# A hybrid decoder layer on one core: a different number of k-pairs by seven products, and partial sums of weights added by transfers

## The chip, the core and the metric

The kernel runs on one NeuronCore of a Trainium2 chip. Five instruction streams run side by side: TensorE (PE, with its weight loads shown as PEld), VectorE (DVE), ScalarE (ACT), GpSimd (POOL) and SyncE (SP, which only issues transfers here). They meet through semaphores. The metric is the device time of one execution in microseconds; the median of three runs is given, with the lowest and the highest beside it.

## The reference, cut to what matters

One layer of a decoder, 256 tokens, width 2048, in float32. What matters here is only which large products there are and what follows what:

```python
proj = h @ w_in[i]                       # x_r, g_r, q, k, v, gate_r, gate_a
...
y_r = y_r @ w_rnn_out[i]                 # 2816 x 2048
o = stick_breaking_attention(q, k, v)
y_a = o... @ w_attn_out[i]               # 2048 x 2048
mix = sigmoid(gate_r) * y_r + sigmoid(gate_a) * y_a
x = x + mix @ w_o[i]
gu = rmsnorm(x, g_ffn[i]) @ w_ffn_gu[i]  # 2048 x 11264
x = x + (silu(g) * u) @ w_ffn_down[i]    # 5632 x 2048
x = x + sigmoid(rmsnorm(x, g_ple[i]) @ w_ple_gate[i]) * (p[i] @ w_ple_proj[i])
```

## The kernel before

**Tiles.** Everything is cut into 128. The 256 tokens are two token tiles (0 and 1); a weight matrix is cut into k-tiles (rows) and into groups of 1024 columns, each group being two halves of 512 columns. A float32 value is split into a high and a low part, and `prod` (L613) multiplies one token tile by one 128 x 512 weight piece in three matmuls: high by high, high by low, low by high (L617, L618, L619). What is a weight in the layer is the moving operand here, and the activations are what PE loads.

**Plain k-tiles and pairs.** A plain k-tile needs four products: two token tiles by two column halves. So two plain k-tiles need eight. Two k-tiles can instead be taken as a pair, as a 2 x 2 block product with seven multiplications. It needs sums of weight pieces (`T1`, `T2`, `T3`, `T4` and the like) and sums of activations, which `half_sums` makes (four sums of 128 columns on DVE, then a split into two parts). `pairs_of(name)` says which pairs of a product are done in this way. The first two pairs go as strings in the list of slots ("11", "T1", "21", "22", "T2", "T3", "T4"; each covers both pairs, so each slot has two products); a further pair goes as ("S", 1, p) to ("S", 4, p), four slots with two, two, two and one products.

**Lists of slots.** A group (1024 columns of one product) follows a list: `SEVEN` has two pairs and twelve plain k-tiles, `SEVEN3` three pairs and ten plain ones, `LONG` is `SEVEN3` with six more, and `ONE` has one pair and ten plain ones. Before the change the recurrent output `ro`, `v`, all eleven groups `gu` of the feed-forward's first product, the down parts `dn0` and `dn1` and the last product `pg` use three pairs; the attention's output `ao` and the output projection `wo` use `SEVEN`; the last down part `dn2` uses `ONE`. `tail()` sets the order of the stages: ro, v, the blocks for q, k and gate_a with the attention between them, ao, wo, gu 0 to 3, dn0, gu 4 to 7, dn1, gu 8 to 10, dn2, pg. Each name other than gu has two groups.

**The stream.** One slot is one chunk of weights, mostly 128 x 1024 (512 KB), loaded by SP (L259). `Stream` brings every chunk through four steps. `dma_to` loads it, into one of 4 buffers `w` for a plain k-tile or one of 29 shared buffers `Q` for a piece of a pair; the chunks of some groups (`EARLY`) are ordered 4.5 chunks ahead. `sum_to` makes the weight sums on DVE (`summed`, where `add` is L269), two chunks ahead of the split. `split_to` splits a chunk four chunks ahead of PE: ACT copies it to the high part (`whi`, L345) and DVE subtracts (`wlo`, L346); there are 5 buffers of each. `group` then issues the products.

**Sums by transfers.** Two of the weight sums are not made by DVE: after T2 is split, `joins` has POOL issue a transfer that adds the weights "21" from HBM onto the tile R (L313, with `accum_op`), and T4 is that tile. For an S pair the same is done with half of S1 onto the tile Y, which is S4. The third sums, T3 (tile "12" plus tile "22") and S3 (one half of the tile S2 plus the other), are made by DVE.

**The start.** The first product (`gtr`) begins with two k-tiles cut into four chunks of 512 columns, 0 to 3, each in a `w` buffer of its own. SP loads them between pieces of x, then the parameters `prm`, and the next chunk, 4, when a buffer is free.

After a group its results leave PSUM: `whole` does four additions on DVE, and what follows belongs to the stage (two further multiply-adds a tile in ao, for instance). Transposes of results (`pend`) are put into the next group from slot 3 on, or from slot 5 in ao, wo and pg. `parts_sums` and `next_mix` make the sums of activations for the pairs of the next product.

Of the kernel before, what the change touches and what calls it, by code (L numbers as in the profile page):

```python
# [162 lines left out]
def tail():  # L163


    def wide(name, w, slots, c=0):
        return [(name, g, w, c + 8 * g, c + 8 * g + 4, slots[g]) for g in range(2)]

    def blocks(*cs):
        return [("blk", b, None, c, None, None) for c, b in cs]  # L170

    def gu(*gs):
        return [("gu", g, "gu", 4 * g, 44 + 4 * g, SEVEN3) for g in gs]

    def dn(q):
        k, p = FQ0[q], FQ0[q] // 2
        slots = [x + k if isinstance(x, int) else (*x[:2], x[2] + p) if isinstance(x, tuple) else x
                 for x in SEVEN3] if FQ[q] == 16 else [x if isinstance(x, int) else x + (p,) for x in ONE(k)]
# [50 lines left out]
DMA_ORDER, DMA_UPTO = dma_order()  # L229
CHUNK_OF = {PLAN[c[0]][0][1:]: j for j, c in enumerate(CHUNKS) if PLAN[c[0]][0][0] == "tok"}  # L230


class Stream:
# [9 lines left out]
    def dma_to(self, n):  # L243
        n = DMA_UPTO[min(n, len(CHUNKS))]
        while self.n_dma < n:
# [18 lines left out]
    def summed(self, key):  # L264
# [4 lines left out]
        add = lambda o, a, b: self.nc.vector.tensor_tensor(o, a, b, ALU.add)  # L269
        if isinstance(mode, tuple):  # L270
            _, i, p = mode
            a, b, y = (*at, ("S", 1, p)), (*at, ("S", 2, p)), (*at, "Y", p)
            if i == 2:
                r[y] = self.quad()
                a, b, y = r.pop(a), r[b], r[y]
                add(y[:, :512], a[:, :512], b[:, 512:])
                add(y[:, 512:], y[:, :512], b[:, :512])
                return y, 1024
            if i == 3:
                b = r.pop(b)  # L280
                add(b[:, 512:], b[:, 512:], b[:, :512])
                return b, 1024
            if i == 4:
                return r.pop(y)[:, 512:], 512
            return r[key], 1024
        g = lambda m: (*at, m)
        if mode == "21":
            return r.pop(key), 1024
        if mode in ("11", "22"):
            return r[key], 1024  # L290
        if mode == "T1":
            r[g("R")], r[g("12")] = r.pop(g("11")), r.pop(key)
            add(r[g("R")], r[g("R")], r[g("12")])
            return r[g("R")], 1024
# [10 lines left out]
    def joins(self, key):  # L305

        *at, mode = key
        if mode == "T2":
            t, c, j = self.raw[(*at, "R")], 0, CHUNK_OF[(*at, "21")]
        else:  # L310
            t, c, j = self.raw[(*at, "Y", mode[2])], 512, CHUNK_OF[(*at, ("S", 1, mode[2]))]
        src = self.w[OFFS[j]:OFFS[j] + P * 1024].rearrange("(p c) -> p c", p=P)
        self.nc.gpsimd.dma_start(t[:, c:], src[:, c:], accum_op=ALU.add)  # L313
# [18 lines left out]
    def split_to(self, n):  # L332
        n = min(n, len(CHUNKS))
        while self.n_split < n:
# [6 lines left out]
            else:  # L341
                t, c = self.raw.pop(j), P * (b - a)
            hi = self.phl.tile([P, 1024], F32R, tag="whi", name=f"whi_{j}")
            lo = self.phl.tile([P, 1024], F32R, tag="wlo", name=f"wlo_{j}")
            self.hi_ins = self.nc.scalar.activation(hi[:, :c], t[:, :c], AF.Copy)  # L345
            self.lo_ins = self.nc.vector.tensor_tensor(lo[:, :c], t[:, :c], hi[:, :c].bitcast(F32), ALU.subtract)  # L346
            res = self.parts.setdefault(i, [])
            for x in range(c // P):
                s = slice(x * P, (x + 1) * P)
                res.append((hi[:, s], lo[:, s], hi, lo, x * P))  # L350
            self.n_split += 1
            if mode == "T2" or isinstance(mode, tuple) and mode[:2] == ("S", 2):
                self.joins(PLAN[i][0][1:])
# [41 lines left out]
def tile_hybrid_block(ctx: ExitStack, tc: tile.TileContext, xT: bass.AP, x: bass.AP, pT: bass.AP,  # L395
# [57 lines left out]
    S_.dma_to(4)  # L453
# [472 lines left out]
    for g in range(2):  # L926
        also = {n - 3 + i: (lambda p: lambda: parts_sums(xg, xsum, p))(p) for i, p in enumerate(pairs_of("v"))} if g else {
# [390 lines left out]
```

## Time and profile before

| | us |
|---|---|
| median of 3 runs | 1870.89 |
| lowest and highest | 1869.47, 1871.41 |
| the profiled execution's own time | 1869.97 |
| its span in the profile | 1868.3 |
| PE, DVE, ACT, POOL busy | 1858.0, 1472.1, 1214.5, 43.7 |

The profiled execution takes 1.67 us more than the span that the profile shows. A row of a group reads: line, engine, operation, what it writes and reads, shapes, count, then busy time and mean of one, then the engine's idle time before such instructions and what ended it. A row of stages gives, for a stretch, its length, each engine's busy time with its count, the granted clock of TensorE, the busy share of the 16 DMA engines and what they moved. A matmul's record is longer than the distance to the next one, since matmuls overlap; distances between starts are what counts.

Counted off by the products' records, the stages begin at: gtr 5.2 us, ro 391.4, v 507.0, blocks and attention 590.8, ao 889.2, wo 975.4, gu0 1063.7, dn0 1234.3, gu4 1319.1, dn1 1487.9, gu8 1572.5, dn2 1698.8, pg 1765.5.

### The profile page before, as it was taken

How to read it: one execution, taken by the hardware profiler on the slowest of the kernel's cores; microseconds unless marked ns; L12 is line 12 of the kernel's file. 1: busy time of each engine (PE TensorE's matmuls, PEld its weight loads, DVE VectorE, ACT ScalarE, POOL GpSimd, SP SyncE). 2: the span in 40 equal slices, each digit the busy share in tenths (PEclk: the TensorE clock that was granted, in tenths of full speed). 3: DMA queues.
4: the chain of work that ended last, by engine and by line, in shares of the span. 5: the costliest groups of instructions: out<-in, count | busy, mean ns of one | idle time of the engine just before them, and what ended most of it. 6: DMA issues, size and time to landing. Idle time of an engine off the chain costs nothing.

```text
span 1868.3 us, 24357 instructions
## 1 busy us (share of the span) xinstructions
PE 1858.0 (99%) x8939; PEld 1563.0 (84%) x8939; DVE 1472.1 (79%) x1819; ACT 1214.5 (65%) x1627; POOL 43.7 (2%) x56
## 2 busy tenths in 40 slices
PE   9999999999999999999999999999999999999998
PEld 7899889888888888888888888888888888888887
DVE  7688887687886576667688888798788898788886
ACT  6587888775555576667565776565556565565774
POOL 0000000000000000000000000000000000000000
PEclk9999999999999999999999999999999999999999
DMA  8546555666656654446566666667555577565564
GB/s 284 183 175 188 190 186 198 250 218 194 242 152 207 191 162 152 165 171 233 157 216 225 220 206 238 229 230 251 203 197 197 197 245 267 175 206 200 176 222 149
DMA packets 108984, 380.53 MB, mean 204 GB/s; under 512 B 12224, under 2 KB 12864, under 8 KB 108864
## 3 DMA queue, kind: packets, MB, share of 16 engines
q1 hardware_dynamic: 101808, 359.82, 53.9%
q0 software_dynamic: 6912, 19.14, 6.2%
q8 instruction: 70, 1.15, 0.2%
q14 instruction: 50, 0.41, 0.1%
q10 hardware_dynamic: 144, 0.01, 0.0%
HBM read 376.82 MB, written 2.10 MB: 203 GB/s over the span
## 4 chain that ended last, share of the span: by engine, by line
PE 96%; DVE 2%; DMA 1%; issue 1%; ACT 0%; SPq 0%; DVEq 0%
PE ps L619 26%; PE ps L618 26%; PE ps L617 26%; PE ps L547 9%; PE ps L551 5%; PE ps L531 1%; PE ps L530 1%; PE ps L529 1%; DVE H L422 1%; DVE wlo L346 1%; PE ps L1193 1%; DMA Q<-in_w_dram 1%; DMA w<-in_w_dram 0%; DVE Q L269 0%; PE ps L974 0%
## 5 line engine op out<-in xcount | busy, mean ns | idle before, releaser
L618 PE MATMUL ps<-wlo,Q 128*128 128x512 f32 x2203 | 858.6, 390 | 0.6 <-DVE wlo L346 0.6
L619 PE MATMUL ps<-whi,Q 128*128 128x512 f32 x2203 | 855.3, 389 | 0.0
L617 PE MATMUL ps<-whi,Q 128*128 128x512 f32 x2203 | 820.0, 391 | 1.3 <-ACT whi L345 0.9
L346 DVE TENSOR_TENSOR wlo<-w,whi 128x1024 fp32r<-128x1024 f32 (+2 forms) x533 | 641.5, 1212 | 226.0 <-ACT whi L345 221.8
L345 ACT ACTIVATE whi<-w 128x1024 fp32r<-128x1024 f32 (+2 forms) x533 | 554.8, 1049 | 258.8 <-PE ps L619 193.8
L618 PEld LDWEIGHTS ps<-wlo,Q 128*128 128x128 f32 x2203 | 414.0, 188 | 85.8 <-DVE wlo L346 1.5
L617 PEld LDWEIGHTS ps<-whi,Q 128*128 128x128 f32 x2203 | 413.0, 188 | 86.7 <-ACT whi L345 1.6
L619 PEld LDWEIGHTS ps<-whi,Q 128*128 128x128 f32 x2203 | 413.7, 188 | 85.0
L345 ACT ACTIVATE whi<-Q 128x1024 fp32r<-128x1024 f32 (+1 forms) x267 | 272.9, 1023 | 261.1 <-PE ps L619 224.5
L346 DVE TENSOR_TENSOR wlo<-Q,whi 128x1024 fp32r<-128x1024 f32 (+1 forms) x267 | 313.8, 1177 | 75.0 <-ACT whi L345 73.3
L547 PE MATMUL ps<-Q,whi 128*128 128x512 f32 x704 | 170.7, 392 | 0.0
L547 PEld LDWEIGHTS ps<-Q,whi 128*128 128x128 f32 x704 | 128.7, 188 | 24.5
L269 DVE TENSOR_TENSOR Q<-Q,Q 128x1024 f32<-128x1024 f32 (+1 forms) x121 | 123.1, 1020 | 20.6 <-DMA Q<-in_w_dram 14.9
L422 DVE TENSOR_TENSOR H<-H,H 128x512 f32<-128x512 f32 (+2 forms) x187 | 106.3, 583 | 6.9 <-ACT H L428 6.5
L428 ACT ACTIVATE H<-ps 128x512 f32<-128x512 f32 (+1 forms) x162 | 83.5, 531 | 43.2 <-PE ps L619 32.6
L422 DVE TENSOR_TENSOR H<-ps,H 128x512 f32<-128x512 f32 (+1 forms) x154 | 88.1, 604 | 14.4 <-PE ps L619 9.6
L551 PEld LDWEIGHTS ps<-Q,wlo 128*128 128x128 f32 x704 | 90.4, 191 | 3.5
L551 PE MATMUL ps<-Q,wlo 128*128 128x256 f32 x704 | 91.5, 283 | 0.0
L313 POOL DMA_DIRECT2D Q<-in_w_dram x48 | 41.1, 857 | 1774.9 <-DVE wlo L346 1771.9
L428 ACT ACT_TABLE_LOAD x53 | 68.0, 1283 | 1.7 <-DVE Q L422 0.7
L428 ACT ACTIVATE Q<-H 128x512 fp32r<-128x512 f32 x54 | 32.8, 623 | 28.0 <-DVE H L422 27.6
L531 PE MATMUL ps<-Q,wlo 128*128 128x256 f32 x140 | 39.6, 283 | 0.0
(122 smaller groups left out, 911.0 us busy)
## 6 DMA issues: line engine op xcount, KB each, us to landing
w<-in_w_dram SPq DMA_DIRECT2D x509, 512.0 KB, 4.3
Q<-in_w_dram SPq DMA_DIRECT2D x146, 512.0 KB, 7.0
Q<-in_w_dram POOLq DMA_DIRECT2D x25, 512.0 KB, 8.2
w<-in_w_dram SPq DMA_DIRECT2D x16, 448.0 KB, 3.2
Q<-in_w_dram POOLq DMA_DIRECT2D x23, 256.0 KB, 4.0
H<-in_x_dram SPq DMA_DIRECT2D x8, 256.0 KB, 5.6
H<-in_xT_dram SPq DMA_DIRECT2D x7, 256.0 KB, 5.5
out_dram<-H SPq DMA_DIRECT2D x7, 256.0 KB, 5.3
```

The costliest lines, as they stand in the source:

```text
L269: add = lambda o, a, b: self.nc.vector.tensor_tensor(o, a, b, ALU.add)
L313: self.nc.gpsimd.dma_start(t[:, c:], src[:, c:], accum_op=ALU.add)
L345: self.hi_ins = self.nc.scalar.activation(hi[:, :c], t[:, :c], AF.Copy)
L346: self.lo_ins = self.nc.vector.tensor_tensor(lo[:, :c], t[:, :c], hi[:, :c].bitcast(F32), ALU.subtract)
L422: nc.vector.tensor_tensor(o, a, b, op)
L428: nc.scalar.activation(o, i, f, **kw)
L531: nc.tensor.matmul(o, wt[1], xh, start=False, stop=stop)
L547: nc.tensor.matmul(pss[e], wt[0], rhs(xs, k), start=(k == 0), stop=(k == n - 1))
L551: nc.tensor.matmul(pss[e][:, :256], wt[1], rhs(xs, k)[:, :256], start=False, stop=False)
L617: nc.tensor.matmul(ps, x[0], wh, start=start, stop=False, skip_group_check=goes_on)
L618: nc.tensor.matmul(ps, x[0], wl, start=False, stop=False, skip_group_check=goes_on)
L619: nc.tensor.matmul(ps, x[1], wh, start=False, stop=stop, skip_group_check=goes_on)
```

## The change

The numbers of pairs change: v takes four (`SEVEN4`), ao and wo take three (`SEVEN3`), the last down part takes two S pairs (`TWELVE`). The third sums go to transfers as well: T3 is tile "12" with "22" added from HBM once T1's sum has been made, and S3 is the tile S2 with its other half added from HBM once S2's sums have been made; DVE no longer makes them, and the buffer of "22" is given up at its own split. `joins` takes the tile, the column from which it adds, and the chunk and column that it reads. At the start chunks 0 and 1 share one `w` buffer and one pair of split buffers, as do 2 and 3 (`HALVES`), and SP issues chunk 4 ahead of `prm`. The sums of activations for v begin one slot earlier, as there are four of them.

```diff
-SEVEN = ["11", "T1", "21", 4, 5, "22", 6, 7, "T2", 8, 9, "T3", 10, 11, "T4", 12, 13, 14, 15]
-def ONE(k):
-    return [("S", 1), ("S", 2), k + 2, k + 3, k + 4, ("S", 3), k + 5, k + 6, ("S", 4), *range(k + 7, k + 12)]
+TWELVE = [("S", 1, 0), ("S", 1, 1), ("S", 2, 0), ("S", 2, 1), 4, 5, ("S", 3, 0), 6, ("S", 3, 1), 7, ("S", 4, 0),
+          ("S", 4, 1), 8, 9, 10, 11]
+SEVEN4 = ["11", ("S", 1, 2), ("S", 1, 3), "T1", ("S", 2, 2), ("S", 2, 3), "21", 8, "T2", "22", ("S", 3, 2), 9,
+          ("S", 3, 3), "T3", 10, ("S", 4, 2), ("S", 4, 3), "T4", 11, 12, 13, 14, 15]
+FOUR = ("v",)
...
-        return [FQ0[q] // 2 + i for i in range(3 if FQ[q] == 16 else 1)]
-    return (0, 1, 2) if name in ("ro", "gu", "v", "pg") else (0, 1)
+        return [FQ0[q] // 2 + i for i in range(3 if FQ[q] == 16 else 2)]
+    return (0, 1, 2, 3) if name in FOUR else (0, 1, 2)
...
-    return (wide("ro", "ro", [LONG] * 2) + wide("v", "in", [SEVEN3] * 2, C_V)
+    return (wide("ro", "ro", [LONG] * 2) + wide("v", "in", [SEVEN4] * 2, C_V)
...
-            + wide("ao", "ao", [SEVEN] * 2) + wide("wo", "wo", [SEVEN] * 2) + gu(0, 1, 2, 3) + dn(0) + gu(4, 5, 6, 7) + dn(1)
+            + wide("ao", "ao", [SEVEN3] * 2) + wide("wo", "wo", [SEVEN3] * 2) + gu(0, 1, 2, 3) + dn(0) + gu(4, 5, 6, 7) + dn(1)
...
+HALVES = (1, 3)
...
-                t = self.p32.tile([P, 1024], F32, tag="w32", name=f"w32_{j}")
-                self.raw[j] = t
+                if j in HALVES:
+                    t = self.raw[j - 1][1][:, 512:]
+                    self.raw[j] = t, None
+                else:
+                    t = self.p32.tile([P, 1024], F32, tag="w32", name=f"w32_{j}")
+                    self.raw[j] = t, t
...
                 add(y[:, :512], a[:, :512], b[:, 512:])
                 add(y[:, 512:], y[:, :512], b[:, :512])
+                self.joins(b, 512, g(("S", 2, p)), 0)
                 return y, 1024
             if i == 3:
-                b = r.pop(b)
-                add(b[:, 512:], b[:, 512:], b[:, :512])
-                return b, 1024
+                return r.pop(g(("S", 2, p))), 1024
...
         if mode == "T1":
...
+            t, o = r[g("R")], r[g("12")] = r.pop(g("11")), r.pop(key)
+            add(t, t, o)
+            self.joins(o, 0, g("22"), 0)
+            return t, 1024
         if mode == "T3":
-            t = r.pop(g("12"))
-            add(t, t, r.pop(g("22")))
-            return t, 1024
+            return r.pop(g("12")), 1024
...
+    def joins(self, t, c, key, a):
+        j = CHUNK_OF[key]
         src = self.w[OFFS[j]:OFFS[j] + P * 1024].rearrange("(p c) -> p c", p=P)
-        self.nc.gpsimd.dma_start(t[:, c:], src[:, c:], accum_op=ALU.add)
+        self.nc.gpsimd.dma_start(t[:, c:], src[:, a:a + 1024 - c], accum_op=ALU.add)
...
-    S_.dma_to(4)
+    S_.dma_to(5)
     nc.sync.dma_start(prm_sb, prm)
...
-        also = {n - 3 + i: (lambda p: lambda: parts_sums(xg, xsum, p))(p) for i, p in enumerate(pairs_of("v"))} if g else {
+        also = {n - 4 + i: (lambda p: lambda: parts_sums(xg, xsum, p))(p) for i, p in enumerate(pairs_of("v"))} if g else {
```

More of the change, by code (lines that the diff above doesn't have):

```diff
@@ L341, in split_to @@
             else:
[L342 to L346, printed above, removed]
+                t, c = self.raw.pop(j)[0], P * (b - a)
+            o = 512 * (j in HALVES)
+            if not o:
+                hi = self.hi = self.phl.tile([P, 1024], F32R, tag="whi", name=f"whi_{j}")
+                lo = self.lo = self.phl.tile([P, 1024], F32R, tag="wlo", name=f"wlo_{j}")
+            else:
+                hi, lo = self.hi, self.lo
+            h, l = hi[:, o:o + c], lo[:, o:o + c]
+            self.hi_ins = self.nc.scalar.activation(h, t[:, :c], AF.Copy)
+            self.lo_ins = self.nc.vector.tensor_tensor(l, t[:, :c], h.bitcast(F32), ALU.subtract)
             res = self.parts.setdefault(i, [])
             for x in range(c // P):
-                s = slice(x * P, (x + 1) * P)
-                res.append((hi[:, s], lo[:, s], hi, lo, x * P))
+                s = slice(o + x * P, o + (x + 1) * P)
+                res.append((hi[:, s], lo[:, s], hi, lo, o + x * P))
             self.n_split += 1
-            if mode == "T2" or isinstance(mode, tuple) and mode[:2] == ("S", 2):
-                self.joins(PLAN[i][0][1:])
+            g = lambda m: (*PLAN[i][0][1:3], m)
+            if mode == "T2":
+                self.joins(self.raw[g("R")], 0, g("21"), 0)
+            elif isinstance(mode, tuple) and mode[:2] == ("S", 2):
+                self.joins(self.raw[g(("Y", mode[2]))], 512, g(("S", 1, mode[2])), 512)
     def need(self, j):
```

24 lines of the change are left out of this document (7 added, 17 removed).

## The prediction

> **What bounds the kernel now.** I read the page first: engines, the chain that ended last, the costliest groups, queues.
>
> ```profile
> span 1868.3 us, 24357 instructions
> PE 1858.0 (99%) x8939; PEld 1563.0 (84%) x8939; DVE 1472.1 (79%) x1819; ACT 1214.5 (65%) x1627; POOL 43.7 (2%) x56
> PE 96%; DVE 2%; DMA 1%; issue 1%; ACT 0%; SPq 0%; DVEq 0%
> L313 POOL DMA_DIRECT2D Q<-in_w_dram x48 | 41.1, 857 | 1774.9 <-DVE wlo L346 1771.9
> q1 hardware_dynamic: 101808, 359.82, 53.9%
> q0 software_dynamic: 6912, 19.14, 6.2%
> Q<-in_w_dram POOLq DMA_DIRECT2D x25, 512.0 KB, 8.2
> Q<-in_w_dram POOLq DMA_DIRECT2D x23, 256.0 KB, 4.0
> ```
>
> PE is 99% busy and 96% of the chain. As a matmul's record overlaps the next, I then took the timeline of PE in ro's second group, to see the true distance, and the waits of PE.
>
> ```profile
> 464.83 0.39 PE L617 MATMUL ps<-whi,Q 128*128 128x512 f32 x1
> ...
> 509.25 0.39 PE L618 MATMUL ps<-wlo,Q 128*128 128x512 f32 x1
> PE ps L463 <- DVE H L460: 1.6, 1, 1.6
> PE ps L617 <- ACT whi L345: 0.9, 1, 0.9
> PE ps L618 <- DVE wlo L346: 0.6, 1, 0.6
> PE ps L617 <- ACT H L428: 0.5, 2, 0.2
> PE ps L1193 <- DVE H L425: 0.2, 1, 0.2
> ```
>
> The first and last of 197 consecutive matmuls stand 44.42 us apart: 0.2266 us each, without a hole. All waits of PE add up to 3.8 us, 1.6 of them the warm-up. So PE sets the end by the number of its matmuls: one fewer is worth 0.227 us wherever its operands come in time.
>
> **The change part by part. Matmuls.** A pair takes seven products in place of eight, and three matmuls make a product. Each group of v, ao, wo and dn2 gets one more pair: 61 to 60 products in v, 62 to 61 in ao and wo, 47 to 46 in dn2. Eight groups, eight products, 24 matmuls: 24 x 0.2266 = **-5.4 us**. That is all the change takes off the bound; the rest is whether operands come in time.
>
> **DVE.** Prices by shape, from the groups kept apart by shape:
>
> ```profile
> L346 DVE TENSOR_TENSOR wlo<-w,whi 128x1024 fp32r<-128x1024 f32 x509 | 618.1, 1223 | 218.0 <-ACT whi L345 213.9 <-PE ps L551 0.3
> L346 DVE TENSOR_TENSOR wlo<-Q,whi 128x512 fp32r<-128x512 f32 x23 | 15.9, 691 | 11.8 <-ACT whi L345 11.8
> L269 DVE TENSOR_TENSOR Q<-Q,Q 128x1024 f32<-128x1024 f32 x75 | 91.6, 1223 | 2.3 <-DMA Q<-in_w_dram 0.9
> L269 DVE TENSOR_TENSOR Q<-Q,Q 128x512 f32<-128x512 f32 x46 | 31.7, 689 | 18.3 <-DMA Q<-in_w_dram 14.0 <-issue 3.8
> L269 DVE TENSOR_TENSOR Q<-Q 128x512 f32<-128x512 f32 x23 | 15.8, 686 | 0.0
> L422 DVE TENSOR_TENSOR H<-H,H 128x128 f32<-128x128 f32 x46 | 12.6, 288 | 0.1
> ```
>
> The third sums leave DVE: T3 is 1.22 us, S3 0.69, so each of the 19 groups that keep `SEVEN3` or `LONG` loses 1.91. One more S pair in place of two plain k-tiles adds splits of 3 x 1.22 + 0.69 less 2 x 1.22, and two half adds, 1.38: +3.29. So ao and wo: 3.29 - 1.22 = +2.07 a group; v: 3.29 - 1.91 = +1.38; dn2: 3.29 - 0.69 = +2.60. New sums of activations: 4 x 0.29 + 0.69 = 1.84 for wo's third pair, about 2.5 (one more add of 0.69) for v's fourth, ao's third and dn2's second. In all -36.3 + 8.3 + 2.8 + 5.2 + 9.3 = -10.7 us of 1472. Of the new sums v's fall beside ro's last chunks, where DVE is idle more than 2 us in 4 (rows of 491 and 495 below), so nothing is charged; ao's and dn2's have no row here that places them, and I take nothing of their 2.5 us each, nor of dn2's 2.60 a group, with 2.5 and 5 as bounds. DVE wins on the whole but loses in ao and wo, where the windows by stage decide (the third busy time is DVE's):
>
> ```profile
> 507.00:549.40 42.40, 41.82 (x185) 34.31 (x184) 35.63 (x36) 24.32 (x26) 1.69 (x2) 1.00 0.47 143
> 931.30:975.40 44.10, 44.10 (x203) 36.41 (x202) 38.86 (x51) 25.68 (x31) 0.85 (x1) 1.00 0.66 227
> 975.40:1019.60 44.20, 44.20 (x204) 36.46 (x203) 38.62 (x45) 24.79 (x29) 0.85 (x1) 1.00 0.62 202
> 1019.60:1063.70 44.10, 44.10 (x204) 36.45 (x203) 40.40 (x55) 30.05 (x45) 0.85 (x1) 1.00 0.74 257
> 1234.30:1277.60 43.30, 42.84 (x192) 34.94 (x191) 41.08 (x45) 25.32 (x29) 1.70 (x2) 1.00 0.66 224
> 1487.90:1531.00 43.10, 42.87 (x192) 34.94 (x191) 40.86 (x44) 25.43 (x29) 1.70 (x2) 1.00 0.65 226
> ```
>
> In ao's second group it is idle 5.24 us now, in wo's groups 5.58 and 3.70. The new work (2.07 + 1.84, 2.07, 2.07) and 0.68 us less of PE leave 0.65, 2.83 and 0.95. That still fits, but a DVE that is 98% full cannot wait for ACT or PE without PE feeling it. If all the slack were usable the cost is 0; if none, 3.91 + 0.68 + 2.75 + 2.75 = 10.1. PE draws on chunks split four ahead, and DVE now is idle by ACT's copy more than by lack of time (213.9 us in the first row above), so I take a place near the low end: **+1.2**.
>
> The other way round at dn0 and dn1: in their first groups PE is short of its window by 0.46 and 0.23 us, with DVE 95% full; these groups lose 1.91 us of DVE each, T3's add among what runs ahead of the late splits. A stall also leaves a matmul's record uncovered, 0.39 - 0.23 = 0.16, once or twice. Both stalls and the like one at pg's start go: **-1.4** (bounds 0 and -2).
>
> **v with four pairs.** Its first group stalls now: 42.40 - 41.82 = 0.58 us. The windows of 4 us around v's start (507) say why.
>
> ```profile
> 491.00:495.00 4.00, 4.00 (x20) 3.30 (x19) 1.23 (x1) 1.06 (x1) 0.00 (x0) 1.00 1.01 412
> 495.00:499.00 4.00, 4.00 (x19) 3.34 (x18) 1.53 (x2) 2.01 (x2) 0.00 (x0) 1.00 1.03 417
> ```
>
> The early loads of v's sums meet ro's last plain chunks; the DMA engines are full (412 to 417 GB/s), DVE starves at 1.23 and 1.53 of 4 us and hands PE a split too late. With four pairs two more 512 KB chunks lie ahead of that point: 2 x 0.524 MB / 0.415 = 2.5 us later at worst. Against it, slots S1 and S2 of the fourth pair give PE four more products, 2.72 us, before the first plain chunk, while DVE needs 2 x 1.22 + 1.38 - 1.91 = 1.92 more. So between -0.75 (the stall goes) and +2.5; I take **+0.7**, nearer to a part of the DMA delay, as that is what started the stall. The Trainium skill (DMA: Bandwidth & Descriptors, Where 436 GB/s comes from) says that HBM binds a core's loads at about 358 GB/s; the rows above exceed that, so they decide here. By its figure, as an estimate, the two chunks would cost 2.9 us in place of 2.5.
>
> **Transfers.** 48 adding transfers become 112: four in each of 23 groups with three pairs, six in v's, four in dn2's. The added ones carry 23.3 MB, so q0's 6.2% grows with its bytes to 13.7%, and the two queues' share from 60 to 68%. POOL issues 64 more at 0.857 us, 55 us on an engine that is idle 98%; an issue waits for the DVE sum before it, and nothing but later adding transfers queues behind it, in the order in which DVE makes their sums. T1's transfer has until T3's split, about ten slots; it took 8.2 us where such a slot is 1.4 to 2.7 us. What hides its bytes is a hole in the DMA at each group's start, seen at gu3 (1191.8):
>
> ```profile
> 1161.00:1165.00 4.00, 4.00 (x19) 3.32 (x18) 2.69 (x3) 3.33 (x4) 0.00 (x0) 1.00 1.02 293
> 1189.00:1193.00 4.00, 4.00 (x20) 3.30 (x19) 4.00 (x5) 2.69 (x3) 0.00 (x0) 1.00 0.00 0
> 1189.01 1.23 DVE L269 TENSOR_TENSOR Q<-Q,Q 128x1024 f32<-128x1024 f32 x1
> ```
>
> The last of the group's three whole-tile sums begins at 1189, T1's before it, so T1's transfer falls into a stretch where the DMA engines do nothing. I price it at **0**. Without that hole it costs 0.786 MB a group x 6.05 us per MB (6.2% of 1868.3 us for 19.14 MB) = 4.8 us.
>
> **The start.**
>
> ```profile
> 2.19 0.43 SPq L452 DMA_DIRECT2D H<-in_xT_dram  x1
> 3.19 0.51 ACT L428 ACTIVATE Q<-H,gm_sb 128x256 fp32r<-128x256 f32 x1 [0.67 <-DMA gm_sb<-in_prm_dram]
> 4.08 0.43 SPq L454 DMA_DIRECT2D prm_sb<-in_prm_dram  x1
> 5.58 0.36 SPq L259 DMA_DIRECT2D w<-in_w_dram  x1
> 11.29 0.39 PE L619 MATMUL ps<-whi,Q 128*128 128x512 f32 x1
> 11.44 1.06 ACT L345 ACTIVATE whi<-w 128x1024 fp32r<-128x1024 f32 x1 [2.46 <-DMA w<-in_w_dram]
> 12.55 1.20 PE L617 MATMUL ps<-whi,Q 128*128 128x512 f32 x4 [0.87 <-ACT whi L345]
> 13.81 0.50 PE L618 MATMUL ps<-wlo,Q 128*128 128x512 f32 x1
> ```
>
> Chunk 4 is issued at 5.58 and lands at 11.4; PE loses (12.55 - 11.29 - 0.23) + (13.81 - 12.55 - 4 x 0.23) = 1.03 + 0.34 = 1.4 us. Now its issue takes `prm`'s place at 4.08, 1.5 us sooner and ahead of `prm` and more of x. I take **-1.2**, between 0 and -1.4. On the other side, a shared buffer could make chunk 0's copy wait for chunk 1, about 1 us; but ACT read half of x's first tile at 3.19 with the other half issued only at 2.19, so halves are told apart.
>
> **Sum**, on the profiled execution: 1869.97 - 5.4 - 1.2 - 1.4 + 0.7 + 1.2 = 1863.9. The median of the runs shown lies 0.9 above that execution; a third of it goes on top: **1864.2**.
>
> **Rivals.** *Slower: the adding transfers collide.* If T1's transfer is issued some 6 us into its group or later, it meets the DMA at 1.02 to 1.03 (row of 1161, as at 495), and each of the 11 gu groups is put back by up to 4.8 us. Half of it may be covered by chunks split ahead: 11 x 2.4 = 26, so 1890. The hole at 1189 speaks against it; the full DMA at 1161 and a landing of 8.2 us speak for it. The Trainium skill (DMA: Bandwidth & Descriptors, Issuing engines are not separate DMA queues) backs this one: issuing from a second engine buys no DMA time, as all run on the same 16 engines. The trace agrees: at 1161 a full share moved 293 GB/s, with adding transfers among it, against 417 at 495 without. Chance 0.09.
>
> *DVE takes over in ao and wo.* If 3.70 us, the least idle time that DVE has now, is what its order needs, the three groups stall by 3.05 + 0.87 + 2.75 = 6.7 in place of 1.2: 1869.7, no change. Chance 0.13.
>
> *v's loads come too late.* The full 2.5 us at v, and the same again in its second group, as two split buffers more are asked for: 1864.2 - 0.7 + 5 = 1868.5. Chance 0.08.
>
> *The change does its sums but frees nothing*, as the stages would be bound by DVE or DMA anyway: against it stand the 197 matmuls without a hole and windows with PE at 100%. I fold it into the second.
>
> **How the numbers follow.** The forecast has 0.70, with 1861.5 to 1867 as its own range. A difference under 0.2% (3.7 us, so 1867.2 to 1874.6) can't be told from no change. Faster: 0.70, less 0.01, and some of the second and third, 0.05: 0.74. Same: 0.16. Slower: the first rival and a little of the second: 0.10. The range that should hold 8 in 10 takes in the second and third rivals' prices and, below, the bounds of the start and of dn's stalls: 1860.5 to 1870.
>
> **What would show it.** 24 fewer L617 to L619 records (2203 to 2195 each); L269's 128x1024 adds down from 75 to 50 and no `Q<-Q` adds; 112 adding transfers; no wait of PE at 11.3 us; idle of PE at v's first group under 2 us; ao's second group and wo at 43.4 us each. It is wrong if gu groups take over 42.4 us (collision), or ao and wo keep 44.1 (DVE).

## The result, and the profile after

The changed kernel takes 1862.66 us, the median of four runs (1862.46 to 1863.37), against 1871.12 for four runs of the kernel before: a ratio of 0.9956 with a 95% interval of 0.9942 to 0.9969, so 0.44% faster. The forecast was 1864.2. The profiled execution took 1862.46 us, with a span of 1860.7 in place of 1868.3.

From the page of the kernel after: the engines, the shares of the chain, the adding transfers' issues, the two queues, and the landing times of the adding transfers.

```profile
span 1860.7 us, 24579 instructions
PE 1851.5 (100%) x8915; PEld 1559.6 (84%) x8915; DVE 1460.1 (78%) x1826; ACT 1230.5 (66%) x1648; POOL 98.5 (5%) x120
PE 96%; DMA 1%; DVE 1%; issue 0%; SPq 0%; ACT 0%
L310 POOL DMA_DIRECT2D Q<-in_w_dram x112 | 95.9, 856 | 1713.0 <-DVE Q L273 551.0
q1 hardware_dynamic: 101808, 359.82, 53.9%
q0 software_dynamic: 16128, 42.47, 13.4%
Q<-in_w_dram POOLq DMA_DIRECT2D x50, 512.0 KB, 6.8
Q<-in_w_dram POOLq DMA_DIRECT2D x62, 256.0 KB, 4.8
```

There are 24 matmuls less, 64 adding transfers more (112 in place of 48), and q0's share rose to 13.4% (13.7% was forecast). DVE lost 12.0 us (10.7 was forecast). The chain still runs along PE by 96%.

The waits of PE in the kernel after:

```profile
PE ps L468 <- DVE H L465: 1.6, 1, 1.6
PE ps L623 <- DVE wlo L348: 1.1, 3, 0.7
```

The warm-up stays at 1.6 us; the rest are three waits, 1.1 us together, all for a split on DVE: one at 12 us, two near the start of v. The waits for ACT are gone.

Where the time came from is best seen by stage. Counted off by the products' records (the first matmul with `whi` of one stage to that of the next), with a column each for two kernels of the experiments below. The row gtr runs to the first block of gate_r (333.1 us in the kernel before), and the 58.30 us from there to ro are the same in all four:

| stage | before | after | sums alone | third sums on DVE |
|---|---|---|---|---|
| gtr | 327.90 | 327.12 | 328.24 | 327.22 |
| ro, each group | 57.80 | 57.80 | 57.80 | 57.80 |
| v, first group | 42.37 | 42.46 | 41.48 | 41.87 |
| v, second group | 41.48 | 40.80 | 41.48 | 40.80 |
| ao | 42.16, 44.10 | 41.48, 43.35 | 42.16, 44.10 | 41.48, 43.37 |
| wo | 44.12, 44.10 | 43.43, 43.33 | 44.12, 44.10 | 44.03, 43.36 |
| gu2, gu3 | 42.43, 42.43 | 42.43, 42.43 | 42.43, 42.43 | 42.39, 42.43 |
| dn0, first group | 43.38 | 42.42 | 43.02 | 43.57 |
| dn1, first group | 43.16 | 42.42 | 42.43 | 43.43 |
| dn2 and pg's first group | 115.74 | 114.14 | 115.90 | 114.22 |
| from 0 to the last product | 1861.24 | 1853.67 | 1859.77 | 1856.10 |

Eight groups with one product less are worth 8 x 0.68 = 5.44 us of the 7.57. The other 2.1 are -0.78 at the start, +0.77 in v's first group (0.09 longer, though it has 0.68 less to do), -0.17 in ao and wo beyond their products, -1.70 in dn0 and dn1 and -0.24 around pg's start.

Windows of the kernel after: gu2, ao's second group, wo's two groups. The columns are those of the prediction's windows; the third busy time is DVE's, the last two numbers are the DMA share and GB/s.

```profile
1145.13:1187.56 42.43, 42.43 (x192) 35.14 (x191) 33.56 (x35) 25.77 (x29) 3.42 (x4) 1.00 0.74 236
929.28:972.63 43.35, 43.35 (x201) 35.89 (x199) 41.68 (x58) 28.32 (x35) 3.41 (x4) 1.00 0.71 236
972.63:1016.06 43.43, 43.43 (x200) 35.85 (x199) 38.57 (x47) 25.52 (x29) 3.43 (x4) 1.00 0.84 265
1016.06:1059.39 43.33, 43.33 (x200) 35.98 (x199) 38.55 (x54) 32.30 (x50) 3.43 (x4) 1.00 0.73 237
```

In ao's second group DVE is busy 41.68 of 43.35 us, 96%, and PE does not stop once: its busy time is the length of the window in all four rows. What the prediction charged there, 1.2 us, did not come.

Two views of the start, after: SP's issues, then PE's timeline.

```profile
4.08 0.43 SPq L263 DMA_DIRECT2D w<-in_w_dram  x1
4.56 0.43 SPq L459 DMA_DIRECT2D prm_sb<-in_prm_dram  x1
```

```profile
11.76 0.39 PE L622 MATMUL ps<-whi,Q 128*128 128x512 f32 x1
12.33 0.50 PE L623 MATMUL ps<-wlo,Q 128*128 128x512 f32 x1 [0.18 <-DVE wlo L348]
12.67 0.40 PE L624 MATMUL ps<-whi,Q 128*128 128x512 f32 x1
```

Chunk 4 is issued at 4.08, and its first product starts at 11.76 where it had to start, 0.22 after the product before. Its second, with `wlo`, is 12.33 - 11.76 - 0.23 = 0.34 late. That leaves 0.45 us (the matmul behind the wait is 0.34 in place of 0.23 from the next); counted in the same way it was 1.48 us before (1.03 + 0.34 + 0.11).

### The profile page after: what moved, and what is told of

Read it like the earlier page. It is cut to its first block, busy times and chain, and to the rows that moved or that the text cites. A ratio compares the mean times of both kernels' runs of the same rounds, so it can differ in the third digit from the quotient of the medians.

```text
span 1860.7 us, 24579 instructions
## 1 busy us (share of the span) xinstructions
PE 1851.5 (100%) x8915; PEld 1559.6 (84%) x8915; DVE 1460.1 (78%) x1826; ACT 1230.5 (66%) x1648; POOL 98.5 (5%) x120
## 3 DMA queue, kind: packets, MB, share of 16 engines
q1 hardware_dynamic: 101808, 359.82, 53.9%
q0 software_dynamic: 16128, 42.47, 13.4%
q8 instruction: 70, 1.15, 0.2%
## 4 chain that ended last, share of the span: by engine, by line
PE 96%; DMA 1%; DVE 1%; issue 0%; SPq 0%; ACT 0%
PE ps L623 26%; PE ps L624 26%; PE ps L622 26%; PE ps L552 9%; PE ps L556 5%; PE ps L536 1%; PE ps L535 1%; PE ps L534 1%; DMA w<-in_w_dram 1%; DVE H L427 1%; DVE wlo L348 1%; PE ps L1198 1%; DMA Q<-in_w_dram 0%; PE ps L979 0%; PE ps L1140 0%
## 5 line engine op out<-in xcount | busy, mean ns | idle before, releaser
L624 PE MATMUL ps<-whi,Q 128*128 128x512 f32 x2195 | 852.0, 389 | 0.0
L622 PE MATMUL ps<-whi,Q 128*128 128x512 f32 x2195 | 802.0, 391 | 0.0
L348 DVE TENSOR_TENSOR wlo<-w,whi 128x1024 fp32r<-128x1024 f32 (+2 forms) x517 | 622.9, 1212 | 208.5 <-ACT whi L347 204.4
L347 ACT ACTIVATE whi<-w 128x1024 fp32r<-128x1024 f32 (+2 forms) x517 | 537.7, 1048 | 221.8 <-PE ps L624 159.6
L347 ACT ACTIVATE whi<-Q 128x1024 fp32r<-128x1024 f32 (+1 forms) x299 | 302.6, 1015 | 290.0 <-PE ps L624 258.9
L348 DVE TENSOR_TENSOR wlo<-Q,whi 128x1024 fp32r<-128x1024 f32 (+1 forms) x299 | 348.0, 1168 | 99.8 <-ACT whi L347 97.9
L310 POOL DMA_DIRECT2D Q<-in_w_dram x112 | 95.9, 856 | 1713.0 <-DVE Q L273 551.0
L273 DVE TENSOR_TENSOR Q<-Q,Q 128x512 f32<-128x512 f32 (+1 forms) x112 | 102.9, 928 | 21.4 <-DMA Q<-in_w_dram 16.0
L427 DVE TENSOR_TENSOR H<-ps,H 128x512 f32<-128x512 f32 (+1 forms) x154 | 88.3, 605 | 17.5 <-PE ps L624 12.5
L556 PE MATMUL ps<-Q,wlo 128*128 128x256 f32 x704 | 91.5, 283 | 0.0
L427 DVE TENSOR_TENSOR Q<-H,Q 128x512 fp32r<-128x512 f32 x59 | 40.3, 689 | 1.0 <-ACT Q L433 1.0
```

Source lines behind the costliest of these rows:

```text
L310: self.nc.gpsimd.dma_start(t[:, c:], src[:, a:a + 1024 - c], accum_op=ALU.add)
L347: self.hi_ins = self.nc.scalar.activation(h, t[:, :c], AF.Copy)
L348: self.lo_ins = self.nc.vector.tensor_tensor(l, t[:, :c], h.bitcast(F32), ALU.subtract)
L427: nc.vector.tensor_tensor(o, a, b, op)
L556: nc.tensor.matmul(pss[e][:, :256], wt[1], rhs(xs, k)[:, :256], start=False, stop=False)
L622: nc.tensor.matmul(ps, x[0], wh, start=start, stop=False, skip_group_check=goes_on)
```

## Experiments

All but the sums alone are variants of the changed kernel, and most were timed once. They are read by stage, as most differences are smaller than a time of the whole can tell; where a kernel keeps a stage's code, the lengths agree within 0.1 us between profiles, but for the first stage, v's first group and pg (0.35, 0.5 and 0.3).

### The third sums alone

The kernel before with T3 and S3 made by adding transfers, issued where T1 and S2 are summed; the old pairs, and `HALVES` empty with `dma_to(4)`. In ao and wo, where the old list has "22" ahead of T2, its buffer is given up at T2's sum. The edit is shown against the kernel before.

```diff
-            t = r.pop(g("12"))
-            add(t, t, r.pop(g("22")))
+            self.joins(o, 0, g("22"), 0)
...
-                add(b[:, 512:], b[:, 512:], b[:, :512])
+                self.joins(b, 512, g(("S", 2, p)), 0)
```

> The kernel before, with only the third sums (T3, S3) made by adding transfers: pairs, chunk order and start as before. Theory (the third sums leave DVE, and that is what ends the stalls where DVE was 95% full): the first groups of dn0 and dn1 go from 43.38 and 43.16 us to 42.4, pg's start gains 0.2, everything else keeps its length (gtr 327.9, ao and wo 44.1, gu 42.4); 1868.0 us by the profiled execution. Rival A (the stalls went for another reason, such as the moved sums of activations): dn0 and dn1 keep 43.4 and 43.2, 1870. Rival B (the 64 more transfers take DMA time that something needs): gu groups above 42.43, time above 1872.

Measured: 1867.8 us in ten runs against 1871.3, ratio 0.9982 (0.9972 to 0.9991). The table above has the stages: dn1's stall went, dn0's went by a third only (43.38 to 43.02), and the stall at v's start went as a whole (42.37 to 41.48), which nobody had expected. No gu group got longer, so rival B fell; rival A fell for dn1 and v. The start was 0.34 longer, though SP's issues stand at the same times as before: chunk 4 came later.

Since dn0 kept a stall that the changed kernel lacks, the same kernel was profiled a second time.

> The third sums alone, word for word as run before, for a second profile: dn0's first group stood at 43.02 us there with one stall left, at 1239.6, while every kernel with the whole change had 42.42. If what ended that stall is the third sums and the rest is the timing of single loads in one execution: 42.4 to 42.9 this time. If the order of loads that comes with the old pairs keeps the stall: 43.0 again.

Measured: 43.00, 42.43 in dn1, 41.48 in v. So it is not chance. The timeline of DVE just ahead of dn0, in the first of the two:

```profile
1228.55 0.69 DVE L281 TENSOR_TENSOR Q<-Q,Q 128x512 f32<-128x512 f32 x1 [1.42 <-DMA Q<-in_w_dram]
```

DVE, which has no time to lose here, waits 1.42 us for a load of an S chunk. In the changed kernel the same sum, at 1223.52, has no such wait, though gu3 and dn0 have the same code in both. What differs is seen in the DMA queues from 1225.4 to 1226.9, while that load is under way:

```profile
q8 instruction: 1, 0.02, 3.9%
q14 instruction: 1, 0.01, 1.3%
```

Two packets of the kind that the page calls instruction, 16 KB and 8 KB, take 0.94 and 0.31 us of DMA engines there, and the load lands 2.78 us after the one ahead of it; in the second profile they stand at the same place, and it is 2.65. In the ten other profiles with three pairs in gu3 and dn0 and the new pairs elsewhere, no such packet falls into this load, and it lands 1.28 to 1.48 us after the one ahead of it (2.08 in one). dn1's load of that kind agrees: 1.25 to 1.42 us without a packet, 1.62 to 1.95 in the six profiles with one of 8 KB. (In the kernel before, where the two packets start 0.4 and 1.0 us later, it is 1.75.) So what is left of dn0's stall is probably such a collision, which other programs have at another place; no run moved the packets.

### The third sums on DVE again, with the new pairs

```diff
-            self.joins(o, 0, g("22"), 0)
...
+            add(t, t, r.pop(g("22")))
...
-                self.joins(b, 512, g(("S", 2, p)), 0)
...
+                add(b[:, 512:], b[:, 512:], b[:, :512])
```

> The changed kernel with T3 and S3 added by DVE again; pairs and start as changed. Theory (DVE could not carry the additional pairs without the transfers): DVE gains 1.2 + 3 x 0.69 = 3.3 us in a group with three pairs. ao's second group, DVE 41.8 of 43.35 us now, gets at least 1.8 us longer; wo's groups (38.6 and 39.6) 0 to 1 each; v's first group (four S) 1.5 to 3; dn0 and dn1 return to 43.4 and 43.2. Total 1866.5 to 1870. Rival (a busy DVE costs PE nothing, the relief was not needed): all stages as in the changed kernel, 1862.5.

The expectation counts three S3 in a group with three pairs; there is one, so DVE gains 1.9 and not 3.3 us. Measured: 1864.48 us, ratio 0.9961 (0.9946 to 0.9976); by the profile 2.43 us more than the changed kernel. dn0 and dn1 have their stalls back (+1.15, +1.01), wo's first group is 0.60 longer, and ao's second is not:

```profile
929.10:972.40 43.30, 43.30 (x200) 35.81 (x199) 41.76 (x58) 28.29 (x35) 1.70 (x2) 1.00 0.70 237
972.40:1016.40 44.00, 43.98 (x200) 35.79 (x199) 41.87 (x50) 25.30 (x29) 1.72 (x2) 1.00 0.70 233
1230.80:1274.40 43.60, 42.99 (x193) 34.97 (x192) 41.39 (x46) 25.05 (x30) 1.70 (x2) 1.00 0.68 223
```

At the same 95 to 96% DVE costs PE nothing in ao's second group, 0.6 in wo's first and 1.15 in dn0's first. So the busy share of a window does not say whether PE stops. What says it is the order of DVE's work ahead of the group. The first three rows are this kernel just ahead of dn0 (1230.13): S3's sum, T3's sum, T1's split. The last is T1's split in the changed kernel, where dn0 begins at 1229.99.

```profile
1227.54 0.69 DVE L273 TENSOR_TENSOR Q<-Q 128x512 f32<-128x512 f32 x1
1229.40 1.23 DVE L273 TENSOR_TENSOR Q<-Q,Q 128x1024 f32<-128x1024 f32 x1 [0.57 <-DMA Q<-in_w_dram]
1231.74 1.22 DVE L350 TENSOR_TENSOR wlo<-Q,whi 128x1024 fp32r<-128x1024 f32 x1
```

```profile
1229.44 1.22 DVE L348 TENSOR_TENSOR wlo<-Q,whi 128x1024 fp32r<-128x1024 f32 x1
```

The two third sums, and 0.57 us for which the second of them waits for its load, stand ahead of a split that is wanted sooner than they are. The split comes 2.30 us later than in the changed kernel, and behind it DVE works without a pause until after PE's two stops (at 1237.6 and 1239.4).

### The price of the transfers in the gu groups

T1's adding transfer made twice (the block 22 then counts twice in T3's weights):

```diff
             self.joins(o, 0, g("22"), 0)
+            self.joins(o, 0, g("22"), 0)
```

> The changed kernel with T1's adding transfer made twice, so that the block 22 counts twice in T3's weights: 25 more transfers of 512 KB, 13.1 MB. Theory (the transfers of the change cost nothing in the gu groups, as the engines stand idle at a group's start): gu groups keep 42.4; ro to v, where the DMA share is full, loses up to 1 us more; total 1862.5 to 1864. Rival (DMA time is the price): 0.524 MB x 6.05 us per MB = 3.2 us a group, 25 groups, half of it covered: 1862.5 + 40 = 1902.

Measured: 1862.37 us, all gu and dn groups as before to 0.05, v's first group 42.23. Windows at gu2's start follow, first of the changed kernel, then of this one, with a row for the whole of gu3; then this one's queues.

```profile
1147.00:1151.00 4.00, 4.00 (x19) 3.33 (x18) 4.00 (x6) 3.68 (x6) 0.86 (x1) 1.00 0.17 29
```

```profile
1147.00:1151.00 4.00, 4.00 (x19) 3.34 (x18) 4.00 (x5) 3.69 (x5) 0.86 (x1) 1.00 0.72 125
1187.35:1229.77 42.42, 42.42 (x192) 35.14 (x191) 36.92 (x52) 27.00 (x32) 3.45 (x4) 1.00 0.80 238
```

```profile
q1 hardware_dynamic: 101808, 359.82, 54.9%
q0 software_dynamic: 19728, 55.58, 17.5%
```

The second transfer fills the hole at the group's start: the share goes from 0.17 to 0.72, and PE is busy without a break as before. 25 more transfers, 13.1 MB, cost nothing: 0.524 MB more in a gu group, where the change itself had added 0.786. The collision rival is out in these groups.

The other run on this question gave no answer. The call for T1's transfer was moved from T1's sum to the split of T2:

```diff
-            self.joins(o, 0, g("22"), 0)
...
+                self.joins(self.raw[g("12")], 0, g("22"), 0)
```

> The changed kernel with T1's adding transfer issued only when T2 is split, behind T2's own, some slots later in each group. Rival (the collision of the prediction: outside the hole at the group's start the transfer takes 2.4 to 4.8 us from the loads): gu groups 44.8 to 47, total 1890 or more. Theory (the DMA engines have room beside the loads over the whole group, and T3's split has a lead): gu groups 42.4 to 42.9, total 1862.5 to 1868.

Measured: 1862.48 us and all stages as in the changed kernel, but POOL's order came out the same, and its issues around gu3 stand at 1169.92, 1181.04, 1191.06 and 1194.65 us, against 1170.31, 1180.95, 1190.97 and 1194.57. T1's transfer for gu3 is the one at 1181.04, where it stood at 1180.95 before. So moving the call did not move the transfer, and what a late one costs was not measured.

### v: what the stall is, and whether the fourth pair pays

With three pairs in v:

```diff
-FOUR = ("v",)
+FOUR = ()
...
-    return (wide("ro", "ro", [LONG] * 2) + wide("v", "in", [SEVEN4] * 2, C_V)
+    return (wide("ro", "ro", [LONG] * 2) + wide("v", "in", [SEVEN3] * 2, C_V)
```

> The changed kernel with three pairs in v in place of four. Theory (the fourth pair of v pays its 1.36 us of matmuls back almost wholly in the stall at v's start, which comes from DMA): v's groups 41.48 and 41.48 in place of 42.46 and 40.80, no stall at v; total 1862.2, no difference that can be told. Rival (the stall in v was there with three pairs before the change and stays): 42.4 and 41.48, total 1863.1.

Measured: 41.48 and 41.48, no stall in v, 1862.14 us. The fourth pair takes 1.36 us of products away and brings 1.66 us of stall into the first group (42.46 where 40.80 is free of it); it is 0.3 us on the wrong side. Windows of 4 us at v's start (506), first of the changed kernel, then with three pairs:

```profile
499.00:503.00 4.00, 4.00 (x19) 3.33 (x18) 2.33 (x3) 1.43 (x2) 0.85 (x1) 1.00 1.03 423
503.00:507.00 4.00, 4.00 (x19) 3.31 (x18) 2.92 (x5) 1.60 (x2) 0.00 (x0) 1.00 1.06 289
507.00:511.00 4.00, 4.00 (x20) 3.30 (x19) 3.04 (x5) 3.46 (x5) 0.77 (x1) 1.00 1.02 416
511.00:515.00 4.00, 3.60 (x15) 2.33 (x13) 4.00 (x6) 2.27 (x3) 0.93 (x2) 1.00 0.84 260
```

```profile
503.00:507.00 4.00, 4.00 (x20) 3.30 (x19) 3.97 (x5) 1.73 (x2) 0.00 (x0) 1.00 1.07 231
507.00:511.00 4.00, 4.00 (x19) 3.34 (x18) 4.00 (x7) 3.49 (x5) 0.00 (x0) 1.00 0.08 14
```

With four pairs the DMA engines are full until 511 and DVE is busy only 2.3 to 3.0 of 4 us; with three they are done at 507, and DVE works through. Next, the loads for the sums of v's first group 8 chunks ahead:

```diff
+EARLY["v", 0] = 8
```

> The changed kernel, with the loads for the sums of v's first group moved 8 chunks ahead in place of 4. Theory (v's stall is a shortage of DMA at the end of ro; the loads of the sums stand behind ro's plain chunks): v's first group 40.8 to 41.6 in place of 42.46, total 1861 to 1861.7. Rival A (the same bytes only move, and ro's last chunks come late instead): the same sum, a stall in ro's second group or v, 1862.5. Rival B (DVE's own work at v's start, adds and splits, is what is late): v stays 42.5.

Measured: 46.04 in v's first group, 1865.84 us, worse than either rival. Then S3 of v's first group by DVE, which takes two transfers of 256 KB away and gives DVE 1.38 us:

```diff
-                self.joins(b, 512, g(("S", 2, p)), 0)
+                if at != ["v", 0]:
+                    self.joins(b, 512, g(("S", 2, p)), 0)
...
+                if at == ["v", 0]:
+                    add(b[:, 512:], b[:, 512:], b[:, :512])
```

> The changed kernel, with the third S sums (S3) of v's first group added by DVE: two adding transfers of 256 KB less there, 2 x 0.69 us more on DVE. Theory (the stall at v's start is DMA time, full from 491 to 511, not DVE): v's first group 41.5 to 42.1 in place of 42.46, no other stage changes. Rival (DVE is short there): 43.2 to 43.9.

Measured: 43.11 us. The theory fell in that form, and the rival's range begins 0.1 us above; but the timeline does not bear the rival out either, as DVE idles ahead of the stall. The timelines of DVE say what both had missed. In the changed kernel:

```profile
504.97 1.22 DVE L348 TENSOR_TENSOR wlo<-Q,whi 128x1024 fp32r<-128x1024 f32 x1
...
508.95 1.83 DVE L273 TENSOR_TENSOR Q<-Q,Q 128x512 f32<-128x512 f32 x2 [0.96 <-DMA Q<-in_w_dram]
```

In the kernel with S3 on DVE, and in the one with the loads 8 ahead:

```profile
506.72 0.69 DVE L273 TENSOR_TENSOR Q<-Q,Q 128x512 f32<-128x512 f32 x1 [1.76 <-DMA Q<-in_w_dram]
507.33 1.22 DVE L352 TENSOR_TENSOR wlo<-Q,whi 128x1024 fp32r<-128x1024 f32 x1
```

```profile
509.55 0.69 DVE L274 TENSOR_TENSOR Q<-Q,Q 128x512 f32<-128x512 f32 x1 [4.62 <-DMA Q<-in_w_dram]
510.15 1.22 DVE L349 TENSOR_TENSOR wlo<-Q,whi 128x1024 fp32r<-128x1024 f32 x1
```

The half sum that waits there belongs to v's *second* group (the row with x2 joins the sum of T2 to it). In the program's own order of DVE, with the numbers of the buffers (4638 is the first group's "11", 5066 and 5156 are S1 and S2 of the second) and with other operations left out, the changed kernel has

```
L273 Q_4638<-Q_4638,Q_4692      T1 of the first group
L348 wlo_4881<-Q_4638,whi_4880  its split
L273 Q_5200<-Q_5066,Q_5156      half a sum of the second group
L273 Q_4638<-Q_4638,Q_4876      T2 of the first group
L348 wlo_4910<-Q_4850,whi_4909  split of S2, first group
```

and with the loads 8 ahead the sum of the second group stands ahead of T1's split and of three operations that end ro; with S3 on DVE it stands ahead of T1's split, too. DVE works its operations off in that order: with S3 on DVE, ACT's copy for T1's split had ended at 504.69, and the split began at 507.33, right behind the sum. So the first group's split, whose data are there, stands behind a sum that is wanted 40 us later and whose load, one of the second group's, is held up in full DMA engines.

Six profiles have v's code and DVE's order of the changed kernel, the load landing now sooner, now later. DVE's wait ahead of that sum was 0.74, 0.83, 0.96, 1.00, 1.17 and 1.21 us in them, and the first group took 42.23, 42.33, 42.46, 42.50, 42.67 and 42.74 us: each time 41.5 us and the wait, to 0.03. (0.74 is the run with T1's transfer twice, 0.96 the changed kernel, 1.21 the run of the section on the start.) The other two orders come near it: 43.11 us with a wait of 1.76, 46.04 with 4.62, so 41.35 and 41.42 without. The wait is thus added to the group whole. What is left over 40.80 without it, 0.6 to 0.7 us, is about the sum's own 0.69, but no run takes that part by itself. With all third sums on DVE the sum stands ahead of the split at 505.07 and has no wait: 41.87. With three pairs those sums are over by 502: 41.48.

The adding transfers do hold the load up. It is issued at 495.4 to 495.6 in three kernels and lands at 508.86 in the changed one, at 506.60 without S3's two transfers of 256 KB, and at 503.83 with all third sums on DVE. A sum of the second group put later in DVE's order should end the stall; that was not tried. What was tried is four pairs in v's second group only, which leaves the first with fewer loads ahead of it:

```diff
-    return (wide("ro", "ro", [LONG] * 2) + wide("v", "in", [SEVEN4] * 2, C_V)
+    return (wide("ro", "ro", [LONG] * 2) + wide("v", "in", [SEVEN3, SEVEN4], C_V)
```

> The changed kernel, with four pairs in v's second group only and three in its first; all else as changed. Theory (the fourth pair pays where the DMA engines are not full): v's groups 41.48 and 40.80 in place of 42.46 and 40.80, 1.0 us less in all, 1861.6 us. Rival A (the loads of the second group meet something else and the stall moves there): 41.48 and 41.5, 1862.3. Rival B (the start of v stays short, whatever the pairs): 42.4 and 40.8, 1862.6.

Measured: 41.48 and 40.80, without a stall in either, as the theory had it; from 0 to the last product 1852.44 against 1853.67 (0.98 of it in v, 0.24 in the first stage). The five runs have a median of 1862.50 us (1861.33 to 1863.18), ratio 0.9956 (0.9943 to 0.997): by time it can't be told from the changed kernel.

### The start

`prm` ahead of chunk 4 again (`dma_to(4)`), with the shared buffers as changed.

> The changed kernel with prm loaded ahead of chunk 4 again; halves in one buffer as changed. Theory (it is the place of chunk 4's issue that shortened the start): the first stage returns to 327.9 us (328.2 in the run with the sums alone), PE waits about 1.4 us more than the 0.45 it waits in the changed kernel. Rival (the shared buffers of the halves did it): 327.0 to 327.2 as in the changed kernel.

Measured: 327.61 us. SP's issues, then PE's timeline:

```profile
4.08 0.43 SPq L459 DMA_DIRECT2D prm_sb<-in_prm_dram  x1
4.56 0.91 SPq L263 DMA_DIRECT2D w<-in_w_dram  x2
```

```profile
11.59 0.50 PE L622 MATMUL ps<-whi,Q 128*128 128x512 f32 x1
12.84 0.50 PE L623 MATMUL ps<-wlo,Q 128*128 128x512 f32 x1 [0.76 <-DVE wlo L348]
```

PE waits 12.84 - 11.59 - 0.23 = 1.02 us for the split of chunk 4, where the changed kernel waits 0.34. So about 0.5 of the 0.78 us hang on `prm`'s place alone (the ten other profiles with the changed start lie between 326.88 and 327.23), and neither expectation had it whole: chunk 4 is issued at 4.56 here, 0.48 later than in the changed kernel, but 1.02 ahead of the kernel before, as the two loads of x that stood between are behind it. That the shared buffers let it go ahead of them is likely, since there are only four `w` buffers, but no run shows it.

### Where more pairs stop paying

Four pairs in ao and wo too:

```diff
-FOUR = ("v",)
+FOUR = ("v", "ao", "wo")
...
-            + wide("ao", "ao", [SEVEN3] * 2) + wide("wo", "wo", [SEVEN3] * 2) + gu(0, 1, 2, 3) + dn(0) + gu(4, 5, 6, 7) + dn(1)
+            + wide("ao", "ao", [SEVEN4] * 2) + wide("wo", "wo", [SEVEN4] * 2) + gu(0, 1, 2, 3) + dn(0) + gu(4, 5, 6, 7) + dn(1)
...
-        at[93 + i] = [(lambda p: parts_sums(ost, osum, p), p)]
+        at.setdefault(92 + i, []).append((lambda p: parts_sums(ost, osum, p), p))
```

> The changed kernel with four pairs in attention's output and the output projection too: one product less in each of their four groups (2.7 us of matmuls), DVE 2.6 us more in each, besides the sums of activations. By DVE's busy time now (36.0, 41.8, 38.6, 39.6 of 41.5, 43.4, 43.4, 43.3 us) ao's second group would need 44.4 to 46 us of DVE in a window of 42.7. Theory (DVE costs nothing as long as its busy time fits, and its excess when it does not): ao's groups 40.8 and 44.4 to 46, wo's 42.7 and 42.7; total 1861.5 to 1863.5. Rival (the prediction's: a group above 95% DVE loses some of its slack): wo's groups 43.5 to 45 too, total 1864 to 1867.

Measured: 1870.9 us, the whole gain lost: ao 42.58 and 44.46, wo 48.07 and 42.67, gu0 45.17 in place of 43.35. Windows of ao's two groups and wo's first, then PE's and ACT's timelines at the longest wait:

```profile
887.96:930.54 42.58, 41.53 (x182) 33.56 (x180) 33.84 (x35) 25.92 (x30) 6.01 (x7) 1.00 0.89 251
930.54:975.00 44.46, 41.69 (x190) 33.51 (x188) 39.50 (x60) 27.80 (x37) 4.29 (x5) 1.00 0.69 219
975.00:1023.07 48.07, 46.20 (x198) 36.25 (x198) 47.12 (x55) 28.67 (x34) 5.83 (x7) 0.96 0.84 252
```

```profile
973.96 0.50 PE L622 MATMUL ps<-whi,Q 128*128 128x512 f32 x1 [2.44 <-ACT whi L347]
```

```profile
972.85 1.06 ACT L347 ACTIVATE whi<-w 128x1024 fp32r<-128x1024 f32 x1 [10.11 <-DMA w<-in_w_dram]
```

ao's second group has the length that was expected of it and another cause: DVE is busy 39.50 of 44.46, and PE waits 2.44 us for a copy whose chunk lands late, after ACT has been idle 10.11 us for it. SP issued that chunk at 961.81, behind seven loads for wo's pairs (957.00 to 960.71). DVE is full in wo's first group (47.12 of 48.07), the one that was to fit. The rival's direction holds there, with 5 us in one group and none in the other.

Four pairs in the 11 gu groups:

```diff
-FOUR = ("v",)
+FOUR = ("v", "gu")
...
-        return [("gu", g, "gu", 4 * g, 44 + 4 * g, SEVEN3) for g in gs]
+        return [("gu", g, "gu", 4 * g, 44 + 4 * g, SEVEN4) for g in gs]
```

> The changed kernel with four pairs in the 11 gu groups too: one product less in each, 11 x 0.68 = 7.5 us of matmuls; DVE 2.6 us more in each where it is busy 33.6 to 36.9 of 42.4. Theory (only PE's count of matmuls bounds these groups): gu groups 41.7, total 1855. Rival (DMA: the fourth pair's loads and adding transfers, 0.5 MB more each group, or a shortage of Q buffers): gu groups 42.4 or more, total 1862 or above.

Measured: 1865.56 us in ten runs, ratio 0.9973 (0.9964 to 0.9983): 2.9 us over the changed kernel. Most gu groups take 42.1 to 42.2 where 41.7 was expected; gu0, gu4 and gu8, and all four groups of dn0 and dn1, are 0.3 to 1.8 us longer than in the changed kernel. Windows of gu2 and dn1's second group, and the waits of PE:

```profile
1145.01:1187.16 42.15, 42.15 (x189) 34.45 (x188) 35.16 (x38) 26.84 (x31) 5.14 (x6) 1.00 0.79 247
1526.77:1570.03 43.26, 42.17 (x185) 34.16 (x184) 35.78 (x39) 23.37 (x25) 4.26 (x5) 1.00 0.83 292
```

```profile
PE ps L623 <- DVE wlo L348: 4.8, 9, 1.0
```

DVE is busy 83% in both windows, and yet the whole kernel has nine waits for its splits, 4.8 us, where the changed kernel has three and 1.1. The theory (PE's count alone bounds these groups) fell. The prices that the rival named were not told apart; what the slots show is that `SEVEN4` asks for seven splits, four half sums and a whole-tile sum ahead of its first plain chunk, where `SEVEN3` asks for five, two and one.

## Why the prediction came out

**The matmuls** (-5.4) came to the digit: 24 records fewer, and 0.68 to 0.77 us less in v's second group and in each group of ao and wo.

**ao and wo** (+1.2) is the term that was mis-sized: it measured -0.17. The step that failed is "That still fits, but a DVE that is 98% full cannot wait for ACT or PE without PE feeling it". The 98% never came: DVE's time in ao's second group was to become 38.86 + 3.91 = 42.77 us and became 41.68, and in wo's groups it became 38.57 and 38.55 where the prediction's sums give 40.69 and 42.47. At the 96% of ao's second group PE felt nothing, nor at 41.76 of 43.30 with the third sums on DVE. Whether it would feel 98%, no run shows. The second rival, at 6.7 us, is out.

**The stalls** (-1.4) came to -1.94, and the cause is the one predicted, "T3's add among what runs ahead of the late splits": with the third sums back on DVE, dn0 and dn1 stall again, with T3 and S3 ahead of T1's split. That the sums alone leave 0.6 us of dn0's stall hangs on a load that lands late, probably because of two packets of instructions.

**v with four pairs** (+0.7) measured +0.77, and that is luck: it is -0.89 for the third sums, which end v's old stall by themselves, and +1.66 for the fourth pair. The prediction put the old stall down to DVE's starving by late loads. But with the sums alone DVE starves as long (1.22 and 1.23 us busy in the windows from 491 and 495, against 1.23 and 1.53 before) and the group has no stall; what is gone is S3 and T3, 1.9 us of a DVE that has no time left behind the starving. For the fourth pair a late load is the cause, but the prediction took it for the first group's, and did not see that DVE stands still at a sum of the second. Its third rival had late loads at 2.5 us, and expected the same in the second group, where there was none.

**The start** (-1.2) measured -0.78. Chunk 4's copy came in time; its split on DVE is still 0.34 late, and a matmul behind it costs 0.11. Of what PE no longer waits, about 0.2 us is lost again at the first products, whose matmuls stand 0.43 us apart up to 7.32 here and up to 6.90 before.

**The transfers at 0** is shown in the gu groups by the doubled transfer. The hole was where the prediction saw it, and half of it was used: T1's transfer for gu3 is issued 6.6 us ahead of the group, and in the window from 4.6 to 0.6 us ahead of it the DMA share is 0.60 where the kernel before had 0.00; in the 4 us behind its start it is still 0.01. In v the transfers were not free: with the third sums on DVE v's first group is 0.59 us shorter (41.87), though DVE has more to do. The prediction's term of v counted the two chunks more, not the transfers. The Trainium skill (DMA: Bandwidth & Descriptors, Issuing engines are not separate DMA queues) says that a second issuing engine buys no DMA time; at v, where the engines are full, the load that lands 2.3 us sooner without two transfers agrees, and in the gu groups there is room for them.

The sum was 1863.9 us for a profiled execution, which took 1862.46. The difference is -1.4 for ao and wo, -0.5 for the stalls, +0.4 for the start and +0.1 for v.

## What to carry to other kernels

Where one engine runs without a hole, an instruction less is worth its distance to the next, and the doubt lies in the handover at a stage's start. A second engine is not priced by its busy share over a stage: 96% cost nothing in one place and 83% up to 1.8 us in another; what decided in the two places that were followed up, v and dn0, is what stands in its order ahead of the stage's first operands, and whether that waits for a load that is not needed yet. Adding transfers were free where the DMA engines idle, and where these are full they held up the loads of whatever came next, so the same edit can pay in a stage's second group and not in its first.

## What the runs showed of the hardware

An adding transfer took the DMA engines about twice as long per byte as a load. In the run with T1's transfer doubled, q0 grew from 13.4% to 17.5% of 16 engines' span for 13.11 MB, so 0.041 x 1860.6 / 13.11 = 5.8 us per MB, against 0.549 x 1860.6 / 359.82 = 2.8 for q1. The windows at v show it, too: at shares of 1.03 and 1.06 the engines moved 423 GB/s in one and 289 in the next.

Loads share the DMA engines with packets of the kind that the page calls instruction, too: a load of 512 KB landed 1.25 to 1.48 us behind the one ahead of it in sixteen of the seventeen cases at dn0 and dn1 that met none, 1.62 to 1.95 where it met one of 8 KB, and 2.65 and 2.78 in two profiles where it met one of 8 and one of 16 KB (1.75 in the kernel before, where these came later). That the packets are the cause is argued from this, not tried.
